# Setup's input matrices in one large tile a round, sixteen weight buffers, the way back in groups of four stored by ScalarE, and the query weights loaded earlier

## The chip, the core and the metric

The kernel is one program on one core of a Trainium2 chip (trn2). The core has five engines with a queue each: TensorE (PE, with its weight loads as PEld), VectorE (DVE), ScalarE (ACT), GpSimd (POOL) and SyncE (SP). The metric is the device time of one execution in microseconds (us); smaller is better.

## What is computed

One layer of an encoder block is applied to 512 prompt tokens and 256 sample tokens with the same weights, all in float32:

```python
x += 1/2 * postnorm(SwiGLU_1(prenorm(x)))                       # macaron half-step FFN
h  = prenorm(x); z = h @ w_in  -> [u_ssm | q_c | kv_c | k_rope]  # one combined input projection
y_ssm = groupnorm(S5 bidirectional complex-diagonal SSM(u_ssm) + GLU)
y_att = groupnorm(bidirectional MLA(q_c, kv_c, k_rope))
x += postnorm(concat(y_ssm, y_att) @ w_out)
x += 1/2 * postnorm(SwiGLU_2(prenorm(x)))
```

The width is 1024, the feed-forward width 2816, the state space model has 32 groups of 16 channels with 64 states and two directions, and the attention has 8 heads, a query rank of 384 and a key-value rank of 256.

## The kernel before, in words

All 768 tokens stay on the chip through three stages: the first feed-forward half (ffn1), the mixing stage (`mix`) and the second feed-forward half (ffn2).

**Feed-forward.** `ffn` walks over 11 pairs of hidden blocks (q = 0 to 10, 256 hidden columns each). Float32 operands are split into a high part (a cast, L99, on ScalarE) and a low part (a subtraction, L100, on VectorE), and a product is three passes with them (L118 to L120, in `down` L126 to L128). The first pair is multiplied plainly; for the other ten `wino` forms the gate and the up projection with seven products instead of eight (`pa`, `pb`, `pe`, `pc`, `pd` are their PSUM tiles, two of them used twice). Before it can multiply, `wino` adds pieces of the raw weights on VectorE: L396 forms s, L397 and L398 overwrite the raw tiles, and L408 another piece. `down(q-1)` multiplies the hidden blocks of the pair before with the down weights: 12 products (`ps_d`, 6 matmuls each), each added to `acc` on VectorE (L454). It is listed between the gate and the up projection of pair q.

**Setup behind ffn1.** `ssm_setup` prepares the state space model's matrices. It is a generator; `behind(background, PACE[1])` lets it advance 0.3 steps for every product of `down`. Its last part is 16 rounds: `product` (three VectorE operations, L673, L675 and L676) forms 128x512 elements, four transposes on PE (`ps_m`, L660) turn them, ScalarE copies them out (L662) and stores them in DRAM as `dM` (L663). What is left when ffn1's products are listed is listed after them, ahead of the last two pairs' `down`.

**Mix.** `mix` projects to u, then query and key-value columns. u goes through DRAM (`dU`, L771) into tiles `U` (L777). `ssm_back`, a second generator behind the mixing stage at pace `KPACE`, forms the matrices of the way back in 16 rounds of two groups: `matrices` (the same three operations of `product`), `kernels` (eight small matmuls into two PSUM banks `ps_k`, L720, each in two passes, and two stores `dO` on SP's queue, L722) and `together` (two ScalarE copies, two VectorE operations L730 and L731, and a store `dK` on SP's queue, L732). The query weights' raw loads (L70, `raw<-in_w_in`) follow the last u projection in the program. A recurrence of 62 steps on GpSimd (L819 to L822) and the attention on PE follow; `ps_y` (L1076) needs the end of the recurrence.

**Order and buffers.** A scheduler that simulates the program fixes the order of each engine's instructions ahead of the run; an engine takes them in that order. Tiles come from pools: `s6` (20 buffers of 6 KB a partition), `w4` (15 of 4 KB) and `t2` (6 of 2 KB); an instruction that first writes a tile waits until the buffer's last user is done. PSUM has four banks `gu`, two `dn` (`ps_d` uses these) and two `bg`.

Of the kernel before, what the change touches and what calls it, by code (L numbers as in the profile page):

```python
# [8 lines left out]
F32 = mybir.dt.float32  # L9
F32R = mybir.dt.float32r  # L10
AF = mybir.ActivationFunctionType
ALU = mybir.AluOpType
# [29 lines left out]
PACE = (2.0, 0.3)  # L42
# [7 lines left out]
class Kernel:  # L50
    N6, N4, N2 = 20, 15, 6
# [473 lines left out]
    def ssm_setup(self):  # L525
# [18 lines left out]
        q = [tC[:, 576 + 256 * x : 832 + 256 * x].rearrange("p (i g) -> p i g", i=8) for x in range(2)]  # L544
        nat = self.t2("lam_nat", [2, 128])
# [105 lines left out]
        W = {}  # L651
        for b in range(17):
            if b < 16:
                W[b] = self.t2("ssm_w", [512])
                self.product(W[b], self.t2("ssm_t", [512]), Bm, QW, 2 * b, 8)
                yield
            if b:
                ps, w = self.bg([128, 4, 128], "ps_m"), W.pop(b - 1)
                for x in range(4):
                    nc.tensor.transpose(ps[:, x, :], w[:, 128 * x : 128 * x + 128], self.ident)  # L660
                stg = self.t2("ssm_stg", [4, 128])
                nc.scalar.copy(stg, ps)  # L662
                nc.scalar.dma_start(self.dM[:, 2 * b - 2 : 2 * b].rearrange("p g r n -> p (g r) n"), stg)  # L663
                yield
# [13 lines left out]
    def ssm_back(self):  # L678
# [12 lines left out]
        dsk = self.small.tile([64, 16], F32, name="dsk")  # L691
        nc.gpsimd.memset(dsk, 0.0)
        for q_ in range(2):
            dma(dsk[32 * q_ : 32 * q_ + 16, :], A["d_skip"][0].rearrange("(b q c) -> q c b", q=2, c=16)[q_])
        mask = self.small.tile([64, 16], F32, name="mask")
        dma(mask, A["c_mask"])
# [10 lines left out]
        def matrices(b):  # L707
            if b % 2 == 0:
                w = self.s6("ssm_w", [2, 576])
                for x in range(2):  # L710
                    CL[b + x] = w[:, x]
            self.product(CL[b], self.w4("ssm_t", [576], F32), CT, PX, 2 * b, 9)
            CL[b] = CL[b].rearrange("p (g r i c) -> p g r i c", g=2, r=2, c=16)

        def kernels(b):
            PS[b] = [self.bg([64, 128], "ps_k") for _ in range(2)]
# [17 lines left out]
        for i in range(16 + 2):  # L734
            for f, lag in ((together, 2), (kernels, 1), (matrices, 0)):
                if 0 <= i - lag < 16:
                    f(i - lag)
            yield
# [548 lines left out]
```

## Time and profile before

| | before |
|---|---|
| median of three runs | 1562.14 us (1560.68 to 1563.74) |
| the profiled execution | 1563.13 us, of which the span from the first to the last instruction is 1561.1 us |
| PE busy | 1436.6 us (92%) |
| VectorE busy | 1039.5 us (67%) |
| ScalarE busy | 584.6 us (37%) |
| GpSimd busy | 271.5 us (17%) |
| TensorE's mean granted clock | 0.960 |

Busy time is the time in which an engine works on an instruction, as a share of the span. A granted clock of 1.00 is the full clock of TensorE. In a row of the timeline the first two numbers are the start and the duration, and the brackets at the end hold the idle time of the engine ahead of the instruction and what ended it. The rows below are from the one profiled execution.

### The profile page before, as it was taken

To read this page: it belongs to the slowest core of one execution; us is meant where nothing else is said; L and a number is where in the kernel's file an instruction comes from. 1 tells how busy PE (TensorE), PEld (TensorE's weight loads), DVE (VectorE), ACT (ScalarE), POOL (GpSimd) and SP (SyncE) were. 2 spreads that over 40 slices of the span, in tenths; PEclk is the share of its full clock that TensorE was granted. 3 is DMA by queue.
4 is the path that set the end of the run, shared out by engine and by line. 5 is a ranking of instruction groups with operands and counts; after the bars stand their busy time and mean duration, and the time that the engine had idled before them with its cause. 6 is when DMAs were issued, how large, how long until landed. Compare 5 with 4: busy or idle time off the path is not lost. (4 is left out here: it accounts for less than half of the span.)

```text
span 1561.1 us, 20390 instructions
## 1 busy us (share of the span) xinstructions
PE 1436.6 (92%) x7820; PEld 1310.4 (84%) x7820; DVE 1039.5 (67%) x1678; ACT 584.6 (37%) x1117; POOL 271.5 (17%) x413
## 2 busy tenths in 40 slices
PE   6999999989889987699799799979999999999997
PEld 6899988889878976688577798778999999999995
DVE  5977878766766877264626364589766677766674
ACT  5442223323322434133376465244422233323231
POOL 1610000000000033010499611434000000000004
PEclk9999999999999999899799899989999999999999
DMA  8122122211222243553402343340221222122123
GB/s 235 38 81 70 66 71 74 95 61 54 68 71 85 77 146 110 137 184 81 115 19 68 109 110 134 120 159 32 82 81 55 69 68 77 58 82 81 55 95 108
DMA packets 116928, 139.76 MB, mean 90 GB/s; under 512 B 32096, under 2 KB 96992, under 8 KB 116832
## 3 DMA queue, kind: packets, MB, share of 16 engines
q1 hardware_dynamic: 114528, 134.27, 28.1%
q10 hardware_dynamic: 2304, 4.20, 0.7%
q8 instruction: 61, 1.00, 0.3%
q14 instruction: 35, 0.29, 0.1%
HBM read 114.57 MB, written 23.09 MB: 88 GB/s over the span
## 5 line engine op out<-in xcount | busy, mean ns | idle before, releaser
L99 ACT CAST w<-raw 128x512 fp32r<-128x512 f32 (+2 forms) x335 | 223.8, 691 | 343.2 <-DVE raw L398 100.0
L100 DVE TENSOR_TENSOR w<-raw,w 128x512 fp32r<-128x512 f32 (+2 forms) x335 | 264.2, 805 | 75.6 <-ACT w L99 74.1
L454 DVE TENSOR_TENSOR acc<-acc,ps_d 128x512 f32<-128x512 f32 x216 | 147.6, 686 | 122.9 <-PE ps_d L128 121.5
L126 PE MATMUL ps_d<-w,hid 128*128 128x512 f32 x528 | 209.5, 398 | 4.3 <-DVE hs L349 2.6
L128 PE MATMUL ps_d<-w,hid 128*128 128x512 f32 x528 | 208.3, 397 | 2.6 <-DVE hid L100 2.6
L127 PE MATMUL ps_d<-w,hid 128*128 128x512 f32 x528 | 209.1, 396 | 0.0
L1193 POOL TENSOR_SCALAR g<-g 128x1024 f32<-128x1024 f32 x2 | 5.6, 2784 | 876.4 <-PE pa L119 456.6
L128 PEld LDWEIGHTS ps_d<-w,hid 128*128 128x128 f32 x528 | 99.7, 189 | 24.9 <-DVE hid L100 3.5
L126 PEld LDWEIGHTS ps_d<-w,hid 128*128 128x128 f32 x528 | 100.6, 191 | 23.0 <-DVE hs L349 3.0
L127 PEld LDWEIGHTS ps_d<-w,hid 128*128 128x128 f32 x528 | 100.6, 191 | 17.5
L118 PE MATMUL pb<-T2h,w 128*128 128x384 f32 x160 | 57.9, 362 | 24.2 <-ACT w L99 24.2
L345 ACT ACTIVATE hs<-hs 128x384 f32<-128x384 f32 x60 | 31.1, 523 | 101.1 <-DVE hs L431 73.3
L99 ACT CAST hid<-hs 128x384 fp32r<-128x384 f32 x88 | 44.6, 512 | 64.6 <-DVE hs L349 55.9
L401 ACT COPY U<-pa 128x384 f32<-128x384 f32 x40 | 19.1, 477 | 113.9 <-PE pa L120 111.6
L119 PE MATMUL pb<-T2l,w 128*128 128x384 f32 x160 | 57.0, 356 | 3.3 <-DVE T2l L273 3.3
L120 PE MATMUL pb<-T2h,w 128*128 128x384 f32 x160 | 57.0, 356 | 0.0
L118 PEld LDWEIGHTS pb<-T2h,w 128*128 128x128 f32 x160 | 32.5, 203 | 27.7 <-ACT w L99 26.7
L118 PE MATMUL pe<-T1h,w 128*128 128x384 f32 x160 | 54.7, 342 | 0.0
L119 PE MATMUL pe<-T1l,w 128*128 128x384 f32 x160 | 54.5, 340 | 0.0
L100 DVE TENSOR_TENSOR hid<-hs,hid 128x384 fp32r<-128x384 f32 x88 | 50.3, 580 | 5.3 <-ACT hid L99 5.3
L119 PE MATMUL pa<-B00l,w 128*128 128x384 f32 x160 | 53.8, 336 | 0.0
L118 PE MATMUL pa<-B00h,w 128*128 128x384 f32 x160 | 53.8, 336 | 0.0
(366 smaller groups left out, 3802.0 us busy)
## 6 DMA issues: line engine op xcount, KB each, us to landing
raw<-in_w_ffn_gate SPq DMA_DIRECT2D x44, 512.0 KB, 4.4
raw<-in_w_ffn_up SPq DMA_DIRECT2D x44, 512.0 KB, 3.6
raw<-in_w_ffn_down SPq DMA_DIRECT2D x44, 512.0 KB, 4.4
x<-in_x_prompt SPq DMA_DIRECT2D x16, 256.0 KB, 7.6
dM<-ssm_stg ACTq DMA_DIRECT2D x16, 256.0 KB, 3.0
dO<-ssm_w SPq DMA_DIRECT2D x32, 128.0 KB, 2.4
raw<-dM SPq DMA_DIRECT2D x8, 512.0 KB, 6.7
raw<-dO SPq DMA_DIRECT2D x8, 512.0 KB, 4.2
```

Source lines behind the costliest of these rows:

```text
L99: self.nc.scalar.copy(hi, src)
L100: (eng or self.nc.vector).tensor_tensor(lo, src, hi.bitcast(F32), op=ALU.subtract)
L118: self.nc.tensor.matmul(ps, A[0][:, k, :], B[0][:, k, :], start=first, stop=False, skip_group_check=True)
L119: self.nc.tensor.matmul(ps, A[0][:, k, :], B[1][:, k, :], start=False, stop=False, skip_group_check=True)
L120: self.nc.tensor.matmul(ps, A[1][:, k, :], B[0][:, k, :], start=False, stop=stop and k == 3, skip_group_check=True)
L126: self.nc.tensor.matmul(ps, lh, rh, start=i == 0, stop=False)
L127: self.nc.tensor.matmul(ps, lh, rl, start=False, stop=False)
L128: self.nc.tensor.matmul(ps, ll, rh, start=False, stop=last)
L345: nc.scalar.activation(hs[:, i, half(nh)], ps, AF.Silu)
L401: nc.scalar.copy(U2, pa)
L454: tt(acc[:, t, sl], acc[:, t, sl], ps, op=ALU.add)
L1193: nc.gpsimd.tensor_scalar(g, g, 0.5, None, op0=ALU.mult)
```

## The change

Four things are changed.

1. In `ssm_setup` each of the 16 rounds takes one `s6` tile of three parts (product, scratch, transposed copy) in place of three `t2` tiles. A round's transposes are listed right behind its product, no longer one round later, and go into the `dn` banks. `PACE[1]` goes from 0.3 to 0.4. `w4` has 16 buffers in place of 15, and `t2` 4 in place of 6.
2. The mask and the skip weights (`mask`, `dsk`) of the way back are loaded at the start of `ssm_setup`, `dsk` by four small loads.
3. The way back runs in 8 rounds of four groups. A round has two products of the same size as before; its 16 small matmuls fill all 128 rows of the two `ps_k` banks, and the loop over the two parts x of a sum is now the outer one, so that neighbouring matmuls write other rows. There are half as many `together` (8), with the same number of operations each on 128 rows; `dO` is stored in 16 pieces of 256 KB (32 of 128 KB before) and `dK` in 8 (16 before), all from ScalarE's queue.
4. The query weights' raw loads are listed ahead of the second half of the u projection, and the first step of `ssm_back` as well. Behind the query projections of the attention the pace is `KPACE` in place of `2 * KPACE`.

The core of the diff:

```diff
-PACE = (2.0, 0.3)
+PACE = (2.0, 0.4)
...
-    N6, N4, N2 = 20, 15, 6
+    N6, N4, N2 = 20, 16, 4
...
+        self.mask, self.dsk = (self.small.tile([128, n], F32, name=z) for z, n in (("mask", 16), ("dsk", 8)))
+        dma(self.mask, A["c_mask"])
+        nc.gpsimd.memset(self.dsk, 0.0)
+        for q_ in range(4):
+            dma(self.dsk[32 * q_ : 32 * q_ + 16, :], A["d_skip"][0].rearrange("(b q c) -> q c b", q=4, c=16)[q_])
...
-        W = {}
-        for b in range(17):
-            if b < 16:
-                W[b] = self.t2("ssm_w", [512])
-                self.product(W[b], self.t2("ssm_t", [512]), Bm, QW, 2 * b, 8)
-                yield
-            if b:
-                ps, w = self.bg([128, 4, 128], "ps_m"), W.pop(b - 1)
-                for x in range(4):
-                    nc.tensor.transpose(ps[:, x, :], w[:, 128 * x : 128 * x + 128], self.ident)
-                stg = self.t2("ssm_stg", [4, 128])
-                nc.scalar.copy(stg, ps)
-                nc.scalar.dma_start(self.dM[:, 2 * b - 2 : 2 * b].rearrange("p g r n -> p (g r) n"), stg)
-                yield
+        for b in range(16):
+            w = self.s6("ssm_w", [3, 512])
+            self.product(w[:, 0], w[:, 1], Bm, QW, 2 * b, 8)
+            yield
+            ps = self.bank("dn", [128, 4, 128], "ps_m")
+            for x in range(4):
+                nc.tensor.transpose(ps[:, x, :], w[:, 0, 128 * x : 128 * x + 128], self.ident)
+            nc.scalar.copy(w[:, 2], ps.rearrange("p x n -> p (x n)"))
+            nc.scalar.dma_start(self.dM[:, 2 * b : 2 * b + 2].rearrange("p g r n -> p (g r n)"), w[:, 2])
+            yield
...
-        def matrices(b):
-            if b % 2 == 0:
-                w = self.s6("ssm_w", [2, 576])
-                for x in range(2):
-                    CL[b + x] = w[:, x]
-            self.product(CL[b], self.w4("ssm_t", [576], F32), CT, PX, 2 * b, 9)
-            CL[b] = CL[b].rearrange("p (g r i c) -> p g r i c", g=2, r=2, c=16)
+        def matrices(b, h):
+            if h == 0:
+                CL[b] = self.s6("ssm_w", [1152])
+            w = slice(576 * h, 576 * h + 576)
+            self.product(CL[b][:, w], self.w4("ssm_t", [576], F32), CT, PX, 4 * b + 2 * h, 9)
 
         def kernels(b):
-            PS[b] = [self.bg([64, 128], "ps_k") for _ in range(2)]
-            for d, (s, i0, o0) in enumerate(((slice(0, 64), 0, 1), (slice(64, 128), 1, 0))):
-                for g in range(2):
-                    for x in range(2):
-                        nc.tensor.matmul(PS[b][d][32 * g : 32 * g + 32], fB[s, x, 32 * b + 16 * g : 32 * b + 16 * g + 32],
-                                         CL[b][s, g, x, i0 : i0 + 8, :].rearrange("p i c -> p (i c)"), start=x == 0, stop=x == 1)
-                dma(self.dO[s, 2 * b : 2 * b + 2].rearrange("p g r n -> p (g r) n"),
-                    CL[b][s, :, :, o0 : o0 + 8, :].rearrange("p g r i c -> p (g r) (i c)"))
-            del CL[b]
+            c = CL.pop(b).rearrange("p (g r i c) -> p g r i c", g=4, r=2, c=16)
+            PS[b] = [self.bg([128, 128], "ps_k") for _ in range(2)]
+            ways = ((slice(0, 64), 0, 1), (slice(64, 128), 1, 0))
+            for x in range(2):
+                for ps, (s, i0, _) in zip(PS[b], ways):
+                    for g in range(4):
+                        c0 = 64 * b + 16 * g
+                        nc.tensor.matmul(ps[32 * g : 32 * g + 32], fB[s, x, c0 : c0 + 32],
+                                         c[s, g, x, i0 : i0 + 8, :].rearrange("p i c -> p (i c)"), start=x == 0, stop=x == 1)
+            for s, _, o0 in ways:
+                nc.scalar.dma_start(self.dO[s, 4 * b : 4 * b + 4].rearrange("p g r n -> p (g r) n"),
+                                    c[s, :, :, o0 : o0 + 8, :].rearrange("p g r i c -> p (g r) (i c)"))
 
         def together(b):
-            ps, KF = PS.pop(b), self.t2("ssm_kf", [240])[0:64]
+            ps, KF = PS.pop(b), self.t2("ssm_kf", [240])
+            stt(KF[:, 112:128], self.mask, self.dsk[:, b : b + 1], ps[0][:, 0:16], op0=ALU.mult, op1=ALU.add)
+            tt(KF[:, 112:128], KF[:, 112:128], ps[1][:, 112:128], op=ALU.add)
             nc.scalar.copy(KF[:, 128:240], ps[0][:, 16:128])
             nc.scalar.copy(KF[:, 0:112], ps[1][:, 0:112])
-            stt(KF[:, 112:128], mask, dsk[:, b : b + 1], ps[0][:, 0:16], op0=ALU.mult, op1=ALU.add)
-            tt(KF[:, 112:128], KF[:, 112:128], ps[1][:, 112:128], op=ALU.add)
-            dma(self.dK[64 * b : 64 * b + 64, :], KF)
-
-        for i in range(16 + 2):
-            for f, lag in ((together, 2), (kernels, 1), (matrices, 0)):
-                if 0 <= i - lag < 16:
-                    f(i - lag)
-            yield
+            nc.scalar.dma_start(self.dK[128 * b : 128 * b + 128, :], KF)
+
+        for i in range(8 + 2):
+            if i >= 2:
+                together(i - 2)
+            if 0 < i < 9:
+                kernels(i - 1)
+            for h in range(2):
+                if i < 8:
+                    matrices(i, h)
+                    yield
+        yield
...
         back, self.free = self.ssm_back(), False
+        next(back)
+        w_q = [columns(512, 2), columns(768, 1)]
         for i in range(4):
             from_h(w_u[i], i, 1, u_done)
             self.behind(back, KPACE)
-        w_q = [*columns(512, 2), *columns(768, 1)]
+        w_q = [op for c in w_q for op in c]
...
-            self.behind(back, 2 * KPACE)
+            self.behind(back, KPACE)
```

What this moves on the engines is shown at three places, as the order of instructions on an engine (names with their buffer's number). The first is VectorE in the pair q = 8 of ffn1, where the up projection's weights are prepared and the 12 products of `down(7)` are added to `acc`. s1_3642 is the `s` of this up projection before, s1_3679 the one after; s1_3787 belongs to the next gate projection. Before:

```order
L454 TENSOR_TENSOR acc_541<-acc_541,ps_d_3613 128x512
L454 TENSOR_TENSOR acc_541<-acc_541,ps_d_3621 128x512
L454 TENSOR_TENSOR acc_541<-acc_541,ps_d_3629 128x512
L673 TENSOR_TENSOR ssm_w_3637<-ssm_a_412 128x512
L675 TENSOR_TENSOR ssm_t_3638<-ssm_a_412,ssm_q_414 128x2x2x128
L396 TENSOR_TENSOR s1_3642<-raw_3373,raw_3375 128x512
L396 TENSOR_TENSOR s1_3787<-raw_3508,raw_3510 128x512
L676 TENSOR_TENSOR ssm_w_3637<-ssm_w_3637,ssm_t_3638 128x512
L397 TENSOR_TENSOR raw_3373<-raw_3373 128x4x128
L397 TENSOR_TENSOR raw_3508<-raw_3508 128x4x128
L398 TENSOR_TENSOR raw_3373<-s1_3642,raw_3373 128x4x128
L100 TENSOR_TENSOR w_3664<-raw_3373,w_3664 128x512
```

After:

```order
L100 TENSOR_TENSOR w_3701<-raw_3407,w_3701 128x512
L413 TENSOR_TENSOR U_3416<-U_3416,pc_3488 128x384
L100 TENSOR_TENSOR w_3718<-s1_3679,w_3718 128x512
L100 TENSOR_TENSOR w_3733<-raw_3409,w_3733 128x512
L100 TENSOR_TENSOR w_3754<-raw_3407,w_3754 128x512
L100 TENSOR_TENSOR hid_3343<-hs_3015,hid_3343 128x384
L100 TENSOR_TENSOR w_3771<-raw_3409,w_3771 128x512
L408 TENSOR_TENSOR raw_3409<-raw_3409,raw_3407 128x4x128
L418 TENSOR_TENSOR hs_3415<-U_3416,pe_3455 128x384
L421 TENSOR_TENSOR hs_3415<-U_3416,pd_3505 128x384
L454 TENSOR_TENSOR acc_549<-acc_549,ps_d_3554 128x512
L100 TENSOR_TENSOR w_3795<-raw_3409,w_3795 128x512
```

Before, L396 to L398 of this up projection and the low part of its first operand (L100) stand behind all 12 adds (L454); now the low parts of the operands made from raw_3407 and s1_3679 stand ahead of the first add.

The second is SP's queue from the first two `dO` stores on. Before:

```order
L722 DMA dO_60<-ssm_w_5164 64x4x128 x2
L777 DMA U_4790<-dU_64 16x16x64 x2
L777 DMA U_4790<-dU_64 16x16x32 x8
L732 DMA dK_63<-ssm_kf_5249 64x240
L722 DMA dO_60<-ssm_w_5164 64x4x128 x2
L732 DMA dK_63<-ssm_kf_5272 64x240
L722 DMA dO_60<-ssm_w_5267 64x4x128 x2
L70 DMA raw_5294<-in_w_in 128x4x256
L70 DMA raw_5296<-in_w_in 128x4x256
L70 DMA raw_5310<-in_w_in 128x4x128
L70 DMA raw_5312<-in_w_in 128x4x128
```

After, the queue from the first u stores (`dU`) on:

```order
L772 DMA dU_64<-uT_4763 128x384
L1230 DMA x1D_57<-x_4777 128x1024
L70 DMA raw_5058<-in_w_in 128x4x256
L772 DMA dU_64<-uT_4763 128x384
L70 DMA raw_5060<-in_w_in 128x4x256
L70 DMA raw_5062<-in_w_in 128x4x128
L70 DMA raw_5064<-in_w_in 128x4x128
L778 DMA U_4765<-dU_64 16x16x64 x6
L772 DMA dU_64<-uT_4764 128x384 x2
```

The query weights' loads (L70, the four `raw<-in_w_in`) stood behind six `dO` and two `dK`; now they stand among the first u stores, and no `dO` or `dK` is left in this queue.

The third is ScalarE's queue ahead of the query weights' casts (L99). Before:

```order
L702 COPY ssm_ct_5099<-ps_c_5121 128x32x16
L770 COPY uT_4788<-ps_5212 128x384
L728 COPY ssm_kf_5249<-ps_k_5196 64x112
L729 COPY ssm_kf_5249<-ps_k_5197 64x112
L728 COPY ssm_kf_5272<-ps_k_5255 64x112
L729 COPY ssm_kf_5272<-ps_k_5256 64x112
L99 CAST w_5298<-raw_5294 128x512
```

After:

```order
L697 COPY ssm_ct_5048<-ps_c_5099 128x32x16
L771 COPY uT_4764<-ps_5203 128x384
L719 DMA dO_60<-ssm_w_5142 64x8x128 x2
L99 CAST w_5244<-raw_5058 128x512
L99 CAST w_5247<-raw_5060 128x512
```

The four copies of the first two `ssm_kf` are gone from this place; two issues of `dO` stand in it.

## Rows read from the trace of the kernel before

**Rows 1.** The page: PE's share, and 40 slices of PE's busy tenths and granted clock.

```profile
PE 1436.6 (92%) x7820; PEld 1310.4 (84%) x7820; DVE 1039.5 (67%) x1678; ACT 584.6 (37%) x1117; POOL 271.5 (17%) x413
...
PE   6999999989889987699799799979999999999997
...
PEclk9999999999999999899799899989999999999999
```

**Rows 2.** Windows: length, PE, PEld, DVE, ACT, POOL busy (count), clock, DMA share, GB/s.

```profile
440.00:480.00 40.00, 33.75 (x177) 31.98 (x176) 29.37 (x49) 13.69 (x24) 0.00 (x0) 0.91 0.25 86
...
640.00:680.00 40.00, 24.57 (x163) 22.30 (x162) 13.43 (x24) 7.68 (x18) 0.00 (x0) 0.74 0.71 216
```

**Rows 3.** PE on tiles pa and pd: ns min/median/max, first and last start; ffn1, then ffn2.

```profile
L118 PE MATMUL pa<-B00h,w x80: 330/335/422, 62.5 to 533.4; 128*128 128x384 f32 x80
...
L118 PE MATMUL pd<-T4h,w x80: 333/334/335, 90.5 to 545.9; 128*128 128x384 f32 x80
...
L118 PE MATMUL pa<-B00h,w x80: 333/335/347, 1076.1 to 1501.8; 128*128 128x384 f32 x80
...
L118 PE MATMUL pd<-T4h,w x80: 333/334/335, 1103.0 to 1514.3; 128*128 128x384 f32 x80
```

**Rows 4.** PE's waits in ffn1, 60 to 560 us: total, times, longest.

```profile
PE pb L118 <- ACT w L99: 24.2, 6, 6.2
PE pb L119 <- DVE T2l L273: 3.3, 1, 3.3
PE ps_d L128 <- DVE hid L100: 2.6, 1, 2.6
PE ps_m L660 <- ACT ssm_stg L662: 0.9, 1, 0.9
PE ps_d L126 <- ACT hid L99: 0.9, 1, 0.9
```

**Rows 5.** PE's waits in ffn2, 1060 to 1530 us.

```profile
PE ps_d L126 <- DVE hs L349: 2.6, 1, 2.6
PE ps_d L126 <- ACT acc L452: 0.8, 1, 0.8
```

**Rows 6.** Timeline of PE, 440 to 457 us.

```profile
443.77 0.60 PE L660 MATMUL ps_m<-ident,ssm_w 128*128 128x128 f32 x4
...
448.12 0.39 PE L128 MATMUL ps_d<-w,hid 128*128 128x512 f32 x1
454.75 0.69 PE L118 MATMUL pb<-T2h,w 128*128 128x384 f32 x1 [6.25 <-ACT w L99]
```

**Rows 7.** Timeline of SP's queue and of VectorE in the same stretch.

```profile
442.58 5.42 SPq L70 DMA_DIRECT2D raw<-in_w_ffn_up  x2
...
450.35 1.29 DVE L396 TENSOR_TENSOR s<-raw 128x512 f32<-128x512 f32 x2
```

**Rows 8.** ScalarE's copies of ps_m, all 16: ns min/median/max, first and last start.

```profile
L662 ACT COPY ssm_stg<-ps_m x16: 567/587/588, 236.2 to 573.2; 128x512 f32<-128x512 f32 x16
```

**Rows 9.** Timeline of PE and VectorE in mix, 643 to 672 us.

```profile
653.41 2.69 PE L720 MATMUL ps_k<-ssm_w,ssm_b 64*32 64x128 f32 x24 [1.69 <-DVE ssm_kf L731]
665.67 0.69 PE L118 MATMUL ps<-B00h,w 128*128 128x384 f32 x1 [9.57 <-ACT w L99]
...
649.71 0.76 DVE L676 TENSOR_TENSOR ssm_w<-ssm_w,ssm_t 128x576 f32<-128x576 f32 x1
```

**Rows 10.** Timeline of SP's queue in mix, 636 to 672 us.

```profile
638.24 2.80 SPq L694 DMA_DIRECT2D dsk<-in_d_skip  x2
...
659.56 1.26 SPq L722 DMA_DIRECT2D dO<-ssm_w  x2
660.86 2.45 SPq L70 DMA_DIRECT2D raw<-in_w_in  x4
```

**Rows 11.** Timeline: the recurrence's first operation, and PE behind its end.

```profile
767.31 0.49 POOL L819 TENSOR_TENSOR rec_a<-XS,lam 128x128 f32<-128x128 f32 x1
...
887.60 1.17 PE L1076 MATMUL ps_y<-XS,raw 128*128 128x96 f32 x4 [9.57 <-DVE XS L1065]
```

More of the change, by code (lines that the diff above doesn't have):

```diff
@@ L690, in ssm_back @@
                 dma(craw[:, ri, :, s], A[f"c_{p}_{d}"][0].rearrange("(b g) c p -> (g c) b p", b=4))
[L691 to L696, printed above, removed]
         yield
@@ L929, in mix @@
             proj(wq, slice(128 * p, 128 * p + 128), qcT, two_heads(qT[p]))
-            self.behind(back, 2 * KPACE)
+            self.behind(back, KPACE)
             steps(1)
@@ L1258, in constants @@
     ck, sk = np.concatenate([cos, cos], 1), np.concatenate([-sin, sin], 1)
-    mask = np.zeros((64, 16), np.float32)
-    for q in range(2):
+    mask = np.zeros((128, 16), np.float32)
+    for q in range(4):
         mask[32 * q + np.arange(16), np.arange(16)] = 1
```

## The prediction, made before the changed kernel ran

> **What bounds the kernel now.** I read the page first. PE is busy 92% of the span [rows 1]; the slices show where the other 8% lie: of 39 us each, the ninth, twelfth and thirteenth (ffn1) are at 8 tenths, the seventeenth and eighteenth (mix) at 7 and 6, and the granted clock is down to 8 and 7 in places of mix. A gain must come from a place where PE waits. The windows put two such places in numbers [rows 2]: 440 to 480 us has 33.75 us of work at a clock of 0.91, and 640 to 680 us has 24.57 us at 0.74, so a stall costs its own length and some slow time behind it. Next, the same code runs twice, and only ffn1 carries the setup. From the first `pa` to the last `pd` ffn1 takes 545.9 - 62.5 = 483.4 us and ffn2 1514.3 - 1076.1 = 438.2 us, with 80 matmuls of each kind in both [rows 3]. The excess is 45.2 us. The waits explain most of it: in that stretch of ffn1 PE waits 24.2 + 3.3 + 2.6 = 30.1 us (the two waits of 0.9 lie behind it), in ffn2 2.6 + 0.8 = 3.4 us [rows 4, 5]. So 26.7 us are stalls; ten of the sixteen `ps_m` groups lie in the stretch and each delays the next product by about 0.4 us (a group takes 0.60 us [rows 6] and its end overlaps the next product; 0.3 or 0.5 would move the sum by 1 us), which is 4.0; the other 14.5 us I put down to the slow clock behind stalls.
>
> The timeline of one stall shows its cause. At 448.12 PE has run the last `ps_d` and then has nothing until `pb` at 454.75, which waits for a cast [rows 6]. The cast waits for VectorE, which forms `s` only at 450.35, behind all adds of `down` and a setup product; SP's load of these weights was held for 5.42 us from 442.58 on, by buffers of `w4` [rows 7]. Six such waits make the 24.2 us, 4.03 each.
>
> In mix PE does small matmuls until about 656 and then waits 9.57 us, to 665.67, for the cast of the query weights [rows 9]. Their loads are issued at 660.86, on SP behind the stores of the way back (the last two begin at 659.56) [rows 10]. The last bound of this stage is the recurrence: it starts at 767.31, and PE stands 9.57 us before `ps_y` at 887.60 [rows 11]. What starts the recurrence earlier is worth its full length; what only empties PE behind it is not.
>
> **Part 1, setup's rounds and the buffers.** VectorE's work is the same (three operations a round), as are the transposes, the copy and the store. What moves is the order: the operands of the up projection are now prepared ahead of the adds, and the `ps_d` are there to fill PE while later operands are made. This is how the scheduler places ffn2 too, where no wait on `pb` is left [rows 5]. I take it that five of the six waits go: 5 x 4.03 = 20.2 us. Their share of the slow time goes with them: 14.5 x 20.2 / 30.1 = 9.7. All sixteen `ps_m` groups now lie in the stretch; the six that come in cost 6 x 0.4 = 2.4 and save the same behind it. There the two waits of 0.9 [rows 4] lose their cause: -1.8. Against this, an `s6` tile a round makes hidden tiles wait, and `ps_m` shares two banks with `ps_d`; ffn2 keeps 3.4 us of waits in such an order, and I give back about one old wait, +4.0. Sum: -20.2 - 9.7 - 1.8 + 4.0 = -27.7. Bounds: no more than 45.2 - 4.0 = 41 us can go; nothing may go; and it may get worse (last rival). I am near the upper end because the order, not a longer transfer, is what stood in row 448.12.
>
> **Part 2, mask and skip weights.** Four `dsk` loads of 1.40 us each (2.80 for two [rows 10]) and the mask now stand early on SP, between the two loads of the first down weights; they leave SP in mix, where they hide behind the u projection. Behind them are the second down load and setup's inputs; the plain pair's products on PE are the cover (the second slice is at 9 [rows 1]). Bounds: 0, and 4 x 1.40 = 5.6 us if that cover were gone. I take +1.
>
> **Parts 3 and 4, the way back and the query weights.** The query loads are now issued among the first u stores, over 20 us earlier, so their landing no longer ends the wait. An added wait is possible: SP holds the load until `w4` has a buffer, and u's stores and the loads of `U` are queued behind it; those are first used with `dM`, whose loads now follow `U` directly, so I cost this at nothing. The next thing late is ScalarE: ahead of the six casts stand two `dO` issues that wait for the first two half products. The second product ended at 649.71 + 0.76 = 650.5 [rows 9]. On SP two stores of 128 KB took 1.26 us to issue [rows 10]; at up to 1.26 each for 256 KB the casts start by 653.0. Meanwhile PE runs a round of 32 passes: at 2.69 / 24 = 0.112 us each [rows 9] until 650.5 + 3.6 = 654.1. PE then goes on with the projection at 654.1 instead of 665.67: -11.6. Sixteen passes fewer are done by then than before (32 against 48) and come later: 16 x 0.112 = +1.8. The later rounds move from SP to ScalarE: 14 more `dO` at 0.63 to 1.26 and 8 `dK` at no more than 0.63 are some 10 to 23 us of issuing, while 16 pairs of copies become 8. ScalarE is busy 7.68 of 40 us in 640 to 680 [rows 2], so I take 0, between -5 (fewer small copies and waits) and +10 (rival 2). Sum: -9.8, carried by the recurrence to `ps_y`; bounds -15 (PE goes on at 650.5) and 0.
>
> **The sum.** -27.7 + 1 - 9.8 = -36.5, so 1563.1 - 36.5 = 1526.6 for an execution like the profiled one. That one is 1.0 above the median of the runs, so I forecast **1526 us**, -2.3%.
>
> **The rivals.**
> 1. *ffn1's stalls stay.* The load's 5.42 us hold [rows 7] was for buffers, and one more of them may not be enough; the setup tile also takes one of the 20 `s6`. For it: that load was late by more than half of the stall behind it. Against: the operands' place in VectorE's order. Only mix gains: 1562.1 - 9.8 + 1 = 1553. Chance 0.14.
> 2. *Mix gains nothing, or the change doesn't do what it says there.* The issuing of the stores sits on ScalarE between its casts and the norms that release the recurrence, and `t2` has four buffers for `ssm_kf`. Then the 9.57 us wait moves to 750 to 767 us. The page of the Trainium skill "DMA: Bandwidth & Descriptors", section "Rules for kernel authors", says that spreading transfers over issuing engines does not help bandwidth and saves only issue time. No row here shows `dO` from ScalarE; by that rule the transfers themselves finish no earlier. Time: 1562.1 - 27.7 + 1 = 1535. Chance 0.17. Both 1 and 2 failing gives 1562 + 1 = 1563, chance 0.05.
> 3. *Better.* The four neighbouring small matmuls write other rows, and if they overlapped fourfold, the 256 passes at 0.112 x 0.74 = 0.083 (24 passes' price at the clock of that window [rows 2]) would cost 5 instead of 21 us: up to 16 off, 1510; all stalls of ffn1 gone gives 1526 - 13 = 1513. The Trainium skill ("TensorEngine Tiling (Array Packing)", section "Key Properties") says that different tiles can load and multiply in parallel; the 0.112 of rows 9 was measured with two neighbouring passes on one tile and shows no overlap, so the rule is open here. Chance 0.08, because the kv stretch also waits for VectorE.
> 4. *Slower: `ps_m` in the banks of `ps_d`.* PE takes its order as it stands. If a `ps_m` waits for its product (3 x 0.76 = 2.3 us [rows 9]) and the next `ps_d` then for ScalarE's copy of 0.59 [rows 8] to free the bank, with 1.8 us of slow clock behind (14.5 us over the eight waits above one microsecond [rows 4]), one group costs 4.7 us; sixteen cost 75, and 1526 becomes 1601. It decides from 36.5 / 16 = 2.3 us a group on. Against it: the other `dn` bank is free meanwhile, and there is other work between `ps_d`. Chance 0.08.
>
> **How the numbers follow.** My forecast's own case has the remaining 0.48. About 0.2% (3 us) is what a measurement of this kernel can tell from no change, so faster is below 1559 and slower above 1565. The forecast, rivals 1, 2 and 3 are faster: 0.87, less 0.01 for the edge of rival 1. Both failing falls within: 0.05. Slower: 0.08 and the same edge, 0.09. The range leaves out rival 4, the double failure and part of rival 3: 1506 to 1556, which takes in the bounds of mix (-15 to 0) with ffn1 at -28 and those of ffn1 down to nothing with mix at -10.
>
> **What would show it.** Right: `pa` to `pd` of ffn1 takes about 457 us (483.4 - 29.9 + 4.0) and the six waits on `pb` shrink to at most two; no `ps_m` behind the last `pd`; PE goes on after the first `ps_k` at about 654 on the old clock, with the first query cast waiting for no load; the recurrence starts some 37 us earlier. Wrong: waits on `pb`, `ps_d` or `ps_m` above 12 us in ffn1 (rivals 1 and 4, told apart by which tile waits), or a recurrence whose start has moved by no more than ffn1 alone did (rival 2).

## The result and the profile after

The changed kernel takes 1520.95 us (median; 1517.13 to 1522.77) against 1562.94 us, a ratio of 0.9721 with a 95% interval of 0.9686 to 0.9757: 42 us less by the medians and 44 by the ratio, where 36 were forecast. The profiled execution took 1520.6 us, its span is 1518.8 us. Its page, PE's line of busy time and the slices of PE's busy tenths and granted clock, as in [rows 1]:

```profile
PE 1420.5 (94%) x7820; PEld 1299.8 (86%) x7820; DVE 1037.9 (68%) x1662; ACT 582.6 (38%) x1101; POOL 270.1 (18%) x413
...
PE   6897898999999998888899899888999999999997
...
PEclk9999898999999998998899899999999999999998
```

The slices of ffn1 from the sixth on are at 9 or 8, but the fourth has fallen to 7: a hole that was not there before. The windows of [rows 2], with one more at that hole (columns: length, busy time of PE, PEld, DVE, ACT, POOL with counts, clock, DMA share, GB/s):

```profile
120.00:160.00 40.00, 26.95 (x125) 23.60 (x124) 27.17 (x87) 5.60 (x12) 0.00 (x0) 0.86 0.17 53
440.00:480.00 40.00, 40.00 (x215) 37.30 (x215) 31.76 (x54) 14.78 (x26) 0.00 (x0) 1.00 0.18 55
640.00:680.00 40.00, 36.65 (x320) 33.78 (x327) 25.16 (x46) 14.82 (x41) 4.73 (x3) 0.98 0.62 188
```

The first of these windows in the kernel before:

```profile
120.00:160.00 40.00, 40.00 (x209) 37.00 (x208) 30.71 (x86) 11.36 (x21) 0.00 (x0) 1.00 0.26 80
```

440 to 480 us is full and at full clock, 640 to 680 has 36.65 us of work instead of 24.57, and 120 to 160 us has lost 13 us. The rows that answer to [rows 3] (ffn1: first `pa`, last `pd`) and PE's longest waits, as in [rows 4]:

```profile
L118 PE MATMUL pa<-B00h,w x80: 333/334/420, 61.9 to 524.2; 128*128 128x384 f32 x80
...
L118 PE MATMUL pd<-T4h,w x80: 334/334/341, 92.1 to 536.7; 128*128 128x384 f32 x80
```

```profile
PE pb L118 <- ACT w L99: 13.1, 1, 13.1
PE ps_d L126 <- ACT hid L99: 6.0, 2, 5.6
PE pb L119 <- DVE T2l L273: 4.1, 1, 4.1
```

From `pa` to `pd` ffn1 takes 536.7 - 61.9 = 474.8 us, 8.6 less than before, where I had expected some 26 less. The six waits on `pb` are gone, and one of 13.1 us has come. The time lies elsewhere, as the marks of the two traces show. The marks are the first `pa` and last `pd` of ffn1 (L118), the last transpose `ps_c` at the end of the u projection, the first operation of the recurrence and the end of the span; the same table for every kernel is used below, each from its one profiled execution.

| us | ffn1, pa to pd | pd to last ps_c | ps_c to recurrence | recurrence to end |
|---|---|---|---|---|
| before | 483.4 | 99.3 | 122.1 | 793.8 |
| changed | 474.8 | 89.5 | 102.9 | 789.7 |
| difference | -8.6 | -9.8 | -19.2 | -4.1 |

In the five kernels that leave ffn1's rounds as they were its stretch lies between 483.4 and 485.8 us, so a microsecond or two in this table tells nothing. The start gave 0.6 us. So the two stretches of ffn1 brought 18 us and not 28, and the way from `ps_c` to the recurrence 19 and not 10. The sum hid errors of opposite sign. The experiments take them apart.

### The profile page after: what moved, and what is told of

Same layout as the page of the kernel before. It is cut to its first block, busy times and chain, and to the rows that moved or that the text cites. A ratio compares the mean times of both kernels' runs of the same rounds, so it can differ in the third digit from the quotient of the medians.

```text
span 1518.8 us, 20321 instructions
## 1 busy us (share of the span) xinstructions
PE 1420.5 (94%) x7820; PEld 1299.8 (86%) x7820; DVE 1037.9 (68%) x1662; ACT 582.6 (38%) x1101; POOL 270.1 (18%) x413
## 5 line engine op out<-in xcount | busy, mean ns | idle before, releaser
L99 ACT CAST w<-raw 128x512 fp32r<-128x512 f32 (+2 forms) x335 | 224.0, 691 | 298.8 <-DVE raw L398 89.4
L100 DVE TENSOR_TENSOR w<-raw,w 128x512 fp32r<-128x512 f32 (+2 forms) x335 | 264.6, 803 | 51.6 <-ACT w L99 36.6
L454 DVE TENSOR_TENSOR acc<-acc,ps_d 128x512 f32<-128x512 f32 x216 | 147.0, 685 | 139.8 <-PE ps_d L128 139.2
L345 ACT ACTIVATE hs<-hs 128x384 f32<-128x384 f32 x60 | 30.9, 524 | 106.7 <-DVE hs L431 90.8
L118 PE MATMUL pb<-T2h,w 128*128 128x384 f32 x160 | 54.9, 343 | 13.1 <-ACT w L99 13.1
L401 ACT COPY U<-pa 128x384 f32<-128x384 f32 x40 | 19.2, 480 | 123.1 <-PE pa L120 106.2
L99 ACT CAST hid<-hs 128x384 fp32r<-128x384 f32 x88 | 44.4, 511 | 56.9 <-DVE hs L349 48.9
L118 PE MATMUL pa<-B10h,w 128*128 128x384 f32 x160 | 54.7, 342 | 1.6 <-ACT U L401 1.6
L120 PE MATMUL pb<-T2h,w 128*128 128x384 f32 x160 | 54.8, 342 | 0.0
L119 PE MATMUL pa<-B10l,w 128*128 128x384 f32 x160 | 54.6, 341 | 0.0
L120 PE MATMUL pa<-B10h,w 128*128 128x384 f32 x160 | 54.4, 340 | 0.0
L118 PE MATMUL pe<-T1h,w 128*128 128x384 f32 x160 | 53.8, 336 | 0.0
L120 PE MATMUL pa<-B00h,w 128*128 128x384 f32 x160 | 53.8, 336 | 0.0
L118 PE MATMUL pa<-B00h,w 128*128 128x384 f32 x160 | 53.8, 336 | 0.0
```

The costliest lines, as they stand in the source:

```text
L99: self.nc.scalar.copy(hi, src)
L100: (eng or self.nc.vector).tensor_tensor(lo, src, hi.bitcast(F32), op=ALU.subtract)
L118: self.nc.tensor.matmul(ps, A[0][:, k, :], B[0][:, k, :], start=first, stop=False, skip_group_check=True)
L119: self.nc.tensor.matmul(ps, A[0][:, k, :], B[1][:, k, :], start=False, stop=False, skip_group_check=True)
L120: self.nc.tensor.matmul(ps, A[1][:, k, :], B[0][:, k, :], start=False, stop=stop and k == 3, skip_group_check=True)
L345: nc.scalar.activation(hs[:, i, half(nh)], ps, AF.Silu)
```

## Experiments: what held the up projection

In the timeline of the kernel before, VectorE forms `s` (L396) right behind the first two operations of a setup product (L673 at 449.15 and L675 at 449.75 us, `s` at 450.35 [rows 7]). VectorE does not stand idle ahead of it; what is late is its place in the order, which the scheduler fixed ahead of the run. `s` is a tile of the pool `t2`, and so are a round's product, scratch and copy.

**s6_lag_bg.** The kernel before with the rounds' tiles out of `t2`; the lag, the `bg` banks, the pace and the pool sizes stay.

```diff
-                W[b] = self.t2("ssm_w", [512])
-                self.product(W[b], self.t2("ssm_t", [512]), Bm, QW, 2 * b, 8)
+                W[b] = self.s6("ssm_w", [3, 512])
+                self.product(W[b][:, 0], W[b][:, 1], Bm, QW, 2 * b, 8)
...
-                stg = self.t2("ssm_stg", [4, 128])
-                nc.scalar.copy(stg, ps)
+                nc.scalar.copy(w[:, 2], ps.rearrange("p x n -> p (x n)"))
```

> The kernel before with one edit: product, scratch and transposed copy of a setup round in one s6 tile; banks, lag, pace and pool sizes of before. Theory: the up projection's s comes from the same t2 pool as setup's rounds, and waits for their buffers; out of t2 the rounds no longer hold it, the six waits on pb (24.2 us) fall below 5 us in all and the kernel takes 20 to 30 us less (ratio 0.981 to 0.987). Rival (the bank or the lag of the rounds held PE): nothing changes, ratio 0.998 to 1.002.

Measured: 1534.6 us, ratio 0.9816 [0.9788, 0.9843]. PE's waits from 60 to 560 us (total, times, longest; of the two on `ps_d`, the one of 3.3 lies behind the last `pd`):

```profile
PE ps_d L126 <- ACT hid L99: 5.6, 2, 3.3
PE pa L118 <- ACT U L401: 3.6, 1, 3.6
PE pb L119 <- DVE T2l L273: 3.5, 1, 3.5
```

No wait of `pb` for a cast is left, and ffn1 takes 453.5 us from `pa` to `pd`: 29.9 us less, which is the 20.2 + 9.7 that I had put down to these waits and the slow clock behind them. The two terms agree too: from the first `pa` to the last `pd` PE's waits fall from 30.1 to 9.5 us, by 20.6, and its busy time from 453.6 to 444.3, by 9.3, with a granted clock of 0.98 in place of 0.96.

**t2_nolag_dn.** The other half: transposes right behind the product, in the `dn` banks, the tiles from `t2`.

```diff
-        for b in range(17):
...
+        for b in range(16):
...
-                ps, w = self.bg([128, 4, 128], "ps_m"), W.pop(b - 1)
...
+            ps = self.bank("dn", [128, 4, 128], "ps_m")
```

> The kernel before with the other half: a round's transposes right behind its product and in the dn banks, but its three tiles from t2 as before. Theory (the t2 pool): the waits on pb stay, 20 us or more, and the time is within 5 us of before. Rival (bank and lag): the waits go, 20 to 30 us less.

Measured: 1563.63 us, ratio 0.9997 [0.9979, 1.0015]. The waits stay:

```profile
PE pb L118 <- ACT w L99: 22.3, 6, 6.2
```

The bank and the lag give nothing.

**s1_own.** The rounds are left as they were, and `s` gets two buffers of its own, taken from the six of `t2`.

```diff
-    N6, N4, N2 = 20, 15, 6
+    N6, N4, N2 = 20, 15, 4
...
-            s1 = self.t2("s1", [4, 128])
+            s1 = self.pool.tile([128, 4, 128], F32, tag="s1", name="s1", bufs=2)
```

> The kernel before with one edit that leaves setup's rounds alone: the s of the weights' preparation gets two buffers of its own, taken from the six of t2 (t2 then has four, the memory is the same). Theory (s waits for a t2 buffer that a setup round holds): the waits on pb fall below 5 us and the time by 20 to 30 us, as with the rounds moved out (ratio 0.981 to 0.987). Rival (the rounds' own waits for their tiles hold VectorE, and the s6 tile freed those): the waits on pb stay and the time is that of before or worse, 0.998 or more.

Measured: 1528.51 us, ratio 0.9788 [0.9743, 0.9832]. PE's waits in ffn1:

```profile
PE pb L119 <- DVE T2l L273: 4.5, 1, 4.5
PE pa L118 <- ACT U L401: 3.7, 1, 3.7
```

The waits are gone with the rounds still in `t2`; ffn1 takes 454.2 us. The kernel takes 34 us less than before, more than the 20 to 30 expected; the stretches behind ffn1 are shorter too (94.6, 119.9 and 789.0 us), for which no run shows a cause. For the waits in ffn1 the cause is settled: `s` shared a pool with the background, and a background round that held its buffers held the weights' preparation. The sixteenth `w4` buffer, to which I had given a share, is in neither kernel. Whether it gives anything was not tried by itself.

## Experiments: what the pace takes back

**setup_only.** The changed kernel with the way back, its stores, its loads and paces, and the query loads of before. The cut shows the query loads, against the changed kernel.

```diff
-        next(back)
-        w_q = [columns(512, 2), columns(768, 1)]
...
-        w_q = [op for c in w_q for op in c]
+        w_q = [*columns(512, 2), *columns(768, 1)]
```

> Setup's rounds, PACE 0.4, 16 w4 and 4 t2 buffers as in the changed kernel; the way back, its stores and the query loads as before. If the parts add up as the two traces show them (first pa to last pd 8.6 us shorter, behind it to the last ps_t 9 us shorter), the kernel takes about 18 us less than before: ratio 0.987 to 0.990, with the one wait of 13 us on pb in it and the 9.6 us wait for the query casts as before. If the whole of the 28 us that I forecast for this part were there, and the mixing stage had given only the rest: ratio about 0.982.

Measured: 1536.81 us, ratio 0.9828 [0.9798, 0.9859], some 26 us less than before. That is the rival's size for the whole, yet with the stretches of the changed kernel: 474.6 us in ffn1 and 89.6 behind it are 8.8 and 9.7 less than before, and another 5.0 lie between `ps_c` and the recurrence (117.1), for which no run shows a cause.

The wait of 13.1 us is here too. The timeline of the changed kernel there, PE, VectorE and SP's queue (start, duration, operation, idle time ahead):

```profile
157.21 0.69 PE L118 MATMUL pb<-T2h,w 128*128 128x384 f32 x1 [13.05 <-ACT w L99]
...
143.55 0.09 DVE L593 MEMSET ssm_c<- 128x32 f32 x1
...
144.49 0.68 DVE L454 TENSOR_TENSOR acc<-acc,ps_d 128x512 f32<-128x512 f32 x1
...
152.19 1.19 DVE L629 TENSOR_SCALAR ssm_q<-ssm_c 64x256 f32<-64x256 f32 x4
153.41 1.29 DVE L396 TENSOR_TENSOR s<-raw 128x512 f32<-128x512 f32 x2
...
129.01 11.41 SPq L70 DMA_DIRECT2D raw<-in_w_ffn_up  x2
```

The last add (L454) of this `down` is at 144.49; then VectorE works through setup's small operations until 153.4 before it forms `s`. They stand at this place because the pace of 0.4 has brought them a pair earlier.

**pace3.** The changed kernel with the old pace.

```diff
-PACE = (2.0, 0.4)
+PACE = (2.0, 0.3)
```

> The changed kernel with PACE 0.3 as before. The one stall of 13 us on pb in ffn1 stands behind some 40 small setup operations on VectorE that the pace of 0.4 has brought ahead of this up projection; at 0.3 they come a pair later, behind its preparation. Theory (the pace costs more than it gives): first pa to last pd 454 us (475 in the changed kernel), about 9 us more behind it, where six rounds are then left: 8 to 14 us less than the changed kernel, ratio 0.963 to 0.968. Rival (the pace is what shortens the way to the first u projection): the rounds left behind cost as much as the stall, ratio 0.971 to 0.974.

Measured: 1512.01 us, ratio 0.9688 [0.9655, 0.9722]. The median is 9 us below that of the changed kernel, at the low end of what was expected and with a ratio just above it; the two intervals overlap. ffn1 takes 451.7 us (23 less than the changed kernel) and the stretch behind it 99.5 (10.0 more): both terms are there, and the stall is the larger. With the 13 us on `pb` most of a second wait goes, that of a later `down` for a hidden tile; the row in the changed kernel and the one with pace 0.3:

```profile
234.28 0.79 PE L126 MATMUL ps_d<-w,hid 128*128 128x512 f32 x1 [5.57 <-ACT hid L99]
```

```profile
212.62 0.50 PE L126 MATMUL ps_d<-w,hid 128*128 128x512 f32 x1 [1.12 <-ACT hid L99]
```

**late_05.** The pace 0.3 until the rounds begin, and 0.5 from there.

```diff
+        self.pace = 0.3
...
-                        self.behind(side, PACE[1])
+                        self.behind(side, self.pace)
...
+        self.pace = 0.5
         for b in range(16):
             w = self.s6("ssm_w", [3, 512])
```

> The changed kernel with a pace of 0.3 until the sixteen rounds begin and 0.5 from there: all rounds in ffn1 and the chain of small operations a pair later. If both terms are real, this has both: pa to pd 455 to 459 us and 45 to 48 us behind it, 15 to 20 us less than the changed kernel, ratio 0.958 to 0.963. Rival (denser rounds hold the products of down, through the two dn banks or VectorE): no better than 0.966.

Measured: 1503.96 us, ratio 0.9633 [0.9597, 0.9669]. ffn1 takes 455.8 us and the stretch behind it 91.5. It is 17 us below the changed kernel, as expected, and 8 below pace3, where the intervals just overlap. The last of setup's small operations in the two kernels (ns min/median/max, first and last start), the changed one first:

```profile
L629 DVE TENSOR_SCALAR ssm_q<-ssm_c x4: 360/370/378, 152.2 to 153.0; 64x256 f32<-64x256 f32 x4
```

```profile
L629 DVE TENSOR_SCALAR ssm_q<-ssm_c x4: 384/389/391, 170.2 to 171.8; 64x256 f32<-64x256 f32 x4
```

They run 18 us later, behind that up projection's preparation, and no wait on `pb` for a cast is left.

## Experiments: what sets the start of the recurrence

**mix_only.** The way back in fours, its stores, mask and skip loads and pace, and the query loads ahead, in the kernel before.

```diff
+        next(back)
+        w_q = [columns(512, 2), columns(768, 1)]
...
-        for i in range(16 + 2):
+        for i in range(8 + 2):
```

> The way back in fours, stored by ScalarE, its mask and skip loads in setup, and the query loads ahead; setup's rounds, pools and pace of before. If the parts add up as the traces show them (13 us at the query casts, 6 from there to the recurrence, 5 behind it), it takes about 24 us less: ratio 0.983 to 0.986, six waits on pb as before. If only the restart of PE counts, as I forecast: 10 us less, ratio 0.993 to 0.995.

Measured: 1545.44 us, ratio 0.9886 [0.9857, 0.9914], between the two: 17 us less. `ps_c` to the recurrence takes 102.1 us (20 less), the rest is as before.

**query_only.** The query loads alone.

```diff
+        w_q = [columns(512, 2), columns(768, 1)]
         for i in range(4):
...
-        w_q = [*columns(512, 2), *columns(768, 1)]
+        w_q = [op for c in w_q for op in c]
```

> The kernel before with the query weights' four loads listed ahead of the second half of the u projection, and nothing else. Theory (the wait of 9.57 us was for the loads behind dO and dK on SP): the wait falls below 2 us and the time by 8 to 11 us, ratio 0.993 to 0.995. Rival (something behind it, the chain of key-value norms, sets the recurrence's start anyway): within 3 us of before, 0.998 to 1.002.

Measured: 1562.47 us, ratio 1.0009 [0.9984, 1.0033]. A miss of the theory: the wait for the query casts is gone, PE goes on 14 us earlier, and the recurrence starts 122.2 us after `ps_c`, as before. On GpSimd the recurrence stands behind the norm factors (L154, L155) of all six token tiles and starts when the sixth is done. The kernel before:

```profile
766.52 0.19 POOL L154 TENSOR_SCALAR r<-ss 128x1 f32<-128x1 f32 x1 [6.99 <-ACT kv L160]
766.79 0.55 POOL L155 TENSOR_TENSOR r<-r,mhalf 128x1 f32<-128x1 f32 x1
767.31 0.49 POOL L819 TENSOR_TENSOR rec_a<-XS,lam 128x128 f32<-128x128 f32 x1
```

What PE does ahead of that shows why it is late. The kernel before, PE's timeline around the transposes of the normed key-value tiles (`ps_t` from `kv`):

```profile
744.72 1.07 PE L720 MATMUL ps_k<-ssm_w,ssm_b 64*32 64x128 f32 x8 [2.15 <-DVE ssm_kf L730]
745.72 0.47 PE L876 MATMUL ps_t<-ident,kv 128*128 128x128 f32 x1
746.53 1.07 PE L720 MATMUL ps_k<-ssm_w,ssm_b 64*32 64x128 f32 x8 [0.34 <-ACT kvT L877]
747.54 0.47 PE L876 MATMUL ps_t<-ident,kv 128*128 128x128 f32 x1
750.16 1.07 PE L720 MATMUL ps_k<-ssm_w,ssm_b 64*32 64x128 f32 x8 [2.15 <-DVE ssm_kf L730]
```

And the kernel with the query loads ahead, the same stretch:

```profile
754.16 1.07 PE L720 MATMUL ps_k<-ssm_w,ssm_b 64*32 64x128 f32 x8 [2.15 <-DVE ssm_kf L730]
755.97 1.07 PE L720 MATMUL ps_k<-ssm_w,ssm_b 64*32 64x128 f32 x8 [0.34 <-ACT kvT L878]
759.59 1.82 PE L720 MATMUL ps_k<-ssm_w,ssm_b 64*32 64x128 f32 x16 [2.15 <-DVE ssm_kf L730]
```

A round of the way back stands in PE's order ahead of the transposes, and its first matmuls wait for VectorE (L730) to free the banks: 750.16 - 744.72 = 5.4 us a round. On ScalarE the square for the norm of a later token tile (L160) stands behind the casts of such transposes (L877 at 748.05, L160 at 748.50 us), so each round delays the norms behind it. A second hold lies on ScalarE itself, ahead of the last two squares: it waits for the weights `w_uq`, whose loads stand on SP among the `dO` stores of the rounds (the first at 753.75 us). The kernel before:

```profile
757.16 0.92 ACT L99 CAST w<-raw 128x512 fp32r<-128x512 f32 x2 [3.12 <-DMA raw<-in_w_uq]
761.50 0.93 ACT L99 CAST w<-raw 128x512 fp32r<-128x512 f32 x2 [2.75 <-DMA raw<-in_w_uq]
764.68 0.92 ACT L99 CAST w<-raw 128x512 fp32r<-128x512 f32 x2 [2.10 <-DMA raw<-in_w_uq]
```

These are 8.0 us of waiting, and 7.8 with the query loads ahead.

**fours_only.** The other half of mix_only: the query loads, and with them the first step of the way back, in their old place. The cut is against the changed kernel.

```diff
-        next(back)
-        w_q = [columns(512, 2), columns(768, 1)]
...
-        w_q = [op for c in w_q for op in c]
+        w_q = [*columns(512, 2), *columns(768, 1)]
```

> The kernel before with the way back in fours, its stores on ScalarE, its mask and skip loads in setup and the smaller pace at the attention's projections; the query loads in their old place. Both together took 17 us off. Theory (the parts add): 6 to 9 us less than before, ratio 0.994 to 0.996, the wait for the query casts shorter because SP no longer holds stores ahead of the loads, and 64-ns passes of the small matmuls down to some 20 ns. Rival (the query loads made all of it, and fours cost ScalarE as much as they save PE): 0.998 to 1.002.

Measured: 1547.49 us, ratio 0.9907 [0.9875, 0.9938]: 15 us less, more than either theory gave. `ps_c` to the recurrence takes 106.7 us. PE still waits 10 us for the query casts. Behind the first of these transposes stand 96 passes of the small matmuls as before, but they are three rounds and no longer six, so half the hand-overs of banks; and ScalarE has no wait for `w_uq` there. The stretch of mix_only, with the query loads too, is another 4.6 us shorter (102.1 against 106.7); the intervals of the two times overlap.

**query_pace.** The rounds of two groups, the stores on SP as before, the query loads ahead, and the way back ahead of the last key-value products.

```diff
-KPACE = 1.3
+KPACE = 2.6
...
+        w_q = [columns(512, 2), columns(768, 1)]
```

> The kernel before with the query loads ahead, as in the run that changed nothing, and KPACE 2.6 instead of 1.3, so that all sixteen rounds of the way back stand ahead of the last key-value products on PE and none between the transposes that feed the norms. Theory (in the kernel before each round of small matmuls between two of these transposes waits for VectorE to free its banks, about 5.4 us a round, and these rounds, not the query weights, set the recurrence's start; fours halve their number): the recurrence starts 8 to 14 us sooner after the last ps_c than the 122 us of before, ratio 0.990 to 0.995. Rival (the way back as a whole, or a lower clock, sets it wherever the rounds stand): 119 us or more, ratio 0.998 to 1.002.

Measured: 1539.58 us, ratio 0.984 [0.9811, 0.9868], more than expected. `ps_c` to the recurrence takes 99.7 us. The last of the small matmuls on PE and the first of these transposes:

```profile
731.73 0.66 PE L720 MATMUL ps_k<-ssm_w,ssm_b 64*32 64x128 f32 x16
734.53 0.47 PE L877 MATMUL ps_t<-ident,kv 128*128 128x128 f32 x1 [2.14 <-DVE kv L871]
```

All sixteen rounds stand ahead of these transposes, where the kernel before runs them until 761 us with transposes from 728 on between them; and the casts of `w_uq` come before 725 us, ahead of all six norms. So it is the place of the rounds that decides, and with the query loads ahead it does in this stage all that the fours do with them. How much of the 22 us comes through PE's banks and how much through ScalarE's wait for `w_uq`, no run tells. (With the old query loads this pace was not tried; nor were fours with a higher pace.)

**sp_stores.** The changed kernel with the way back's stores issued by SP.

```diff
-                nc.scalar.dma_start(self.dO[s, 4 * b : 4 * b + 4].rearrange("p g r n -> p (g r) n"),
+                dma(self.dO[s, 4 * b : 4 * b + 4].rearrange("p g r n -> p (g r) n"),
...
-            nc.scalar.dma_start(self.dK[128 * b : 128 * b + 128, :], KF)
+            dma(self.dK[128 * b : 128 * b + 128, :], KF)
```

> The changed kernel with dO and dK issued by SP as before (in its sizes of now). Theory (a store's issuing engine matters little, the transfers share the DMA engines and PE waits for neither): within 4 us of the changed kernel, ratio 0.969 to 0.975. Rival (SP's queue, where the stores wait for products and hold the loads of dM and of the key-value weights behind them, cost the 6 us between the restart and the recurrence): 5 to 10 us more than the changed kernel, 0.975 to 0.979.

Measured: 1521.75 us, ratio 0.9753 [0.9719, 0.9787]. The interval overlaps that of the changed kernel, the medians differ by 0.8 us, and `ps_c` to the recurrence takes 101.8 us (102.9). The ratio lies just above what the theory gave, so a loss of a few us isn't excluded, but the recurrence does not start later. The Trainium skill ("DMA: Bandwidth & Descriptors", section "Rules for kernel authors"), which I had cited, says that spreading transfers over issuing engines does not help bandwidth and only saves issue time. The 0.8 us agree with it.

**x_inner.** The changed kernel with the two parts of a sum next to each other.

```diff
-            for x in range(2):
-                for ps, (s, i0, _) in zip(PS[b], ways):
-                    for g in range(4):
+            for ps, (s, i0, _) in zip(PS[b], ways):
+                for g in range(4):
+                    for x in range(2):
```

> The changed kernel with the two parts x of a small product next to each other again (32 rows of PSUM written twice in a row). Theory (small matmuls on different rows overlap): 32 passes take over 2.5 us against 1.70 in the changed kernel's first round, and the stage grows by 2 to 6 us, ratio 0.973 to 0.976. Rival (no overlap, or PE isn't what limits there): the same within 2 us.

Measured: 1519.28 us, ratio 0.9734 [0.9706, 0.9763], the same as the changed kernel: the order of the loops is worth nothing, and the theory that the overlap comes from it is out. The first round takes 1.73 us (1.70 in the changed kernel, over 2.5 by the theory). Its row for a round at full clock and the next matmul, then the same two rows of the changed kernel:

```profile
670.71 0.71 PE L716 MATMUL ps_k<-ssm_w,ssm_b 64*32 64x128 f32 x32
671.35 0.44 PE L119 MATMUL ps<-B01l,w 128*128 128x384 f32 x1
```

```profile
671.43 0.67 PE L716 MATMUL ps_k<-ssm_w,ssm_b 64*32 64x128 f32 x32
672.03 0.44 PE L118 MATMUL ps<-B01h,w 128*128 128x384 f32 x1
```

PE is free again after 0.64 and after 0.60 us: 20 and 19 ns a pass.

## Why the prediction was right, and where it was not

- **The sum.** 1526 us was forecast and 1521 measured, inside the range. The two halves add: setup_only took 26 us off and mix_only 17, together 43, and the whole change 42. The forecast had 27.7 and 9.8 for them. That it came out so near is in part luck: ffn1 fell 15 us short of its part (8.6 less, 23.5 forecast), and the stretches behind it gave 19 more than theirs, of which no run explains the 5.0 between `ps_c` and the recurrence in setup_only nor the 4.1 behind it. One of the prediction's own signs of being wrong came up, a wait above 12 us on `pb`, and neither of the rivals that it names for it (1 and 4) was the cause.
- **Part 1, the waits on `pb`.** The price of the old waits was right: 29.9 us by the sum, 29.9 measured where only the rounds' tiles were changed (s6_lag_bg), and nearly so in each term (20.6 of waits, 9.3 of busy time). Their cause was read half. I named the order on VectorE and the buffers of `w4`; the runs show that the order came from `t2`, which `s` shared with the rounds (s1_own).
- **Part 1, "one old wait" given back, +4.0.** This was the step that failed. The pace of 0.4 was given no term of its own but the six `ps_m` groups; it also moved setup's small operations ahead of an up projection's preparation, which gave a wait of 13.05 us. In ffn1 pace 0.3 leaves 451.7 us and 0.4 474.8. Of the wait of 5.57 us on `ps_d`, 4.5 are the pace's too, since pace 0.3 alone leaves 1.12 of it. (The 457 us that the prediction names for ffn1 leave out its own +2.4 for the six groups.)
- **Part 1, the stretch behind the last `pd`.** -4.2 were forecast (2.4 + 1.8), -9.8 measured to `ps_c`. Pace 0.3 gives 10.0 of it back, so this is the other side of the pace: six rounds less behind ffn1's products are worth some 1.7 us each, and not 0.4. What they hold up there, no run tells.
- **Part 2.** +1 was forecast. The four loads took 2.65 us together on SP, not 5.6. With them the first `pa` starts between 60.7 and 64.6 us in the kernels here, without them between 59.9 and 64.4: no cost shows.
- **Parts 3 and 4, the restart at 654.1.** The mechanism was wrong. In the changed kernel PE goes on 13 us sooner, near the 11.6 worked out (from 20.5 us behind `ps_c` to 7.1), but alone this gives nothing (query_only): its gain is lost before the recurrence. My sentence that the shift is "carried by the recurrence" skipped what stands between; the rounds between the key-value transposes set that start. Waits of `ps_k` for L730 were in the trace of before, 2.15 us each, and I had counted them as "fewer small copies and waits", at no more than 5.
- **Rival 1** (stalls stay) is out: the six are gone in each kernel with `s` and the rounds in different pools. **Rival 2** (mix gains nothing) is out: mix_only is 17 us faster. **Rival 4** (`ps_m` in the banks of `ps_d`) is out: in the changed kernel PE has no wait on a `ps_m`, and in ffn1 its waits on `ps_d` are for hidden tiles. **Rival 3** is half true: small matmuls do overlap (below), but not through the order of the loops, and PE's time on them was not the bound.
- **A reading.** The slices of [rows 1] that the prediction counts as the ninth, twelfth and thirteenth and as the seventeenth and eighteenth are the ninth, eleventh and twelfth and the sixteenth and seventeenth. Nothing rests on it.
- **What stays open.** The stretch from the recurrence to the end is 4.1 us shorter in the changed kernel; it lies between 789.0 and 795.0 us in all kernels here, with no edit in its own code, and no run tells a cause.

## What to carry to other kernels

When a background job shares a buffer pool with the main path's small tiles, it sets the main path's pace, and a table of waits names only the engine that came last: ask of each late instruction which buffer it needed first. A pace for background work has two sides, what is left behind the loop and what is put in front of the loop's own preparation, and one number for a chain of unlike steps may be right for one part and wrong for another. And before a wait that was removed is booked as gain, follow the chain to the next thing that needs it: here 14 us of earlier start alone were worth nothing, with the rounds of small matmuls still in between.

## What the runs showed of the hardware

The passes of the small matmuls (64 rows, 32 columns of weights, 128 columns moved) overlap with each other. A round of two groups, at full clock, with the instruction that follows, in query_pace:

```profile
670.60 0.66 PE L720 MATMUL ps_k<-ssm_w,ssm_b 64*32 64x128 f32 x16
671.19 1.13 PE L806 MATMUL ps_x<-U,raw 128*128 128x96 f32 x8
```

These 16 passes hold PE for 0.59 us, and the 32 of a round of four groups for 0.60 us (671.43 to 672.03 in the changed kernel). The same time does twice the passes where a round spreads over twice as many parts of the array (eight of 64x32, not four). That it isn't a fixed price of a round shows where the scheduler has split one after four passes. By the order of the loops these lie on one part in x_inner and on two in the changed kernel; x_inner first:

```profile
654.28 0.62 PE L716 MATMUL ps_k<-ssm_w,ssm_b 64*32 64x128 f32 x4
654.83 1.13 PE L808 MATMUL ps_x<-U,raw 128*128 128x96 f32 x8
```

```profile
654.26 0.41 PE L716 MATMUL ps_k<-ssm_w,ssm_b 64*32 64x128 f32 x4
654.60 1.13 PE L808 MATMUL ps_x<-U,raw 128*128 128x96 f32 x8
```

Four passes hold PE for 0.55 us on one part and for 0.34 on two. That agrees with the Trainium skill, "TensorEngine Tiling (Array Packing)", section "Key Properties": different tiles can multiply in parallel. The 0.112 us a pass of [rows 9], on which I had built, was measured at a granted clock of 0.50 (653 to 656 us of the kernel before; that is 1.2 of 2.4 GHz), not at the 0.74 of the longer window, so the 0.083 that I took for full clock was too high: here it is 0.037 us a pass on four parts and 0.019 on eight.
